# Hybrid encoder trunk on one core: in the first pass, the stores of operands and values move from SyncE's queue to ScalarE's

## The chip, the cores and the metric

The kernel runs on one core of one Trainium2 chip. The metric is the device time of one execution in microseconds (us), lower is better; the time of before is the median of 3 runs. The engines are TensorE (PE, with its weight loads PEld), VectorE (DVE), ScalarE (ACT), GpSimd (POOL) and SyncE (SP). SP only issues DMA transfers. ACT computes, and can issue them too.

## The reference, cut to what matters

One encoder layer, for a sequence of 2048 and one of 4096 tokens, width 1024:

```python
h = rms_norm(x, pre_g)
proj = einsum('bsd,de->bse', h, w_in)
a_u, a_v, a_gate, b_in, b_gate, c_in, c_gate = split(proj)
ya = mixer_a(a_u, a_v, ...) * silu(a_gate)   # v = layer_norm(gelu(a_v)), 128x128 mix of positions
yb = mixer_b(b_in, b_w, b_scale) * silu(b_gate)   # pooled means
yc = mixer_c(c_in, c_w) * silu(c_gate)   # 2-D Fourier transform
y = einsum('bse,ed->bsd', concat(ya, yb, yc), w_out)
out = x + rms_norm(y, post_g)
```

## The kernel before, in words

**Passes.** The 6144 tokens are 12 blocks of 512. The first pass (0 to about 505 us) takes block after block: it normalises x, projects the columns of a_v, c_in and c_gate, and writes three things to DRAM: the operands of the projections (`op_d`), the values gelu(a_v) (`vn_d`) and the Fourier input and gate (`z_d`, `gc_d`). The later passes read `op_d` and `vn_d` again for the B and A columns, and a last one makes the output. Only the first pass is touched here.

**A block of the first pass.** The 2x2 split of the projection is done with seven products instead of eight, in the order P1, P2, X1, X2, Y1, X3, Y2. Each product takes one operand of 128x1024, in two parts: ACT casts the high part (`p_P1h`, `p_X1h`, ..., L131; L807 in the first block), DVE or POOL subtracts it from the operand to get the low part (`p_P1l`, ..., L132; L805). PE multiplies them in three units (`Pc`, `Xc`, `Yc` twice, `Pg`, `Xg`, `Yg` once). ACT and DVE then evacuate the banks (`ks1c`, `ku2c`, `ku3c`, `s1g`, `cgt`), ACT does the gelu (`vg`, L743, L757) and the silu of the gate (`cgt`, L1003). There are buffers for three operand pairs.

**Where operands come from.** The four quarters of the next block's x (`xp_{b+1}_0..3`) are normalised in place by DVE (L608), after ACT has squared rows of x (`xrow`, L575) and DVE and PE have spread the factor (`diag`, `prb`, `rbc`). Sums and differences of quarters (L171 to L185) overwrite them for X1, X2, Y1, Y2. Each of the seven operands of a block is stored in full, 512 KB: P1, P2 and X3 by `normaliser` (L612), the others by `operands`, all through `keep_operand` (L599). That is 84 stores; the 48 stores of values (192 KB each) stand at L1002.

**What sets the order.** A scheduler places the instructions, except the start-up of block 0, whose order on PE, DVE, ACT and POOL is written out by hand (L829 to L915). Each engine takes its instructions in order, SP its DMAs too: one that must wait holds all behind it. Every DMA signals its end on one of eight semaphores (DMAHW0 to DMAHW7), given out in turn over all DMAs of the program, and waits on that semaphore before it is issued.

Of the kernel before, what the change touches and what calls it, by code (L numbers as in the profile page):

```python
# [15 lines left out]
P = 128  # L16
# [15 lines left out]
def hybrid_encoder(  # L32
# [33 lines left out]
    nc = tc.nc  # L66
# [40 lines left out]
    op_d = dpool.tile([NB, 7, P, 1024], F32, name="op_d")  # L107
    vn_d = dpool.tile([NTOK // P, P, 384], F32, name="vn_d")
# [12 lines left out]
    def chunk(b, c):  # L121


        return b // 2 * SB + c // 2 * TB + b % 2 * HB + c % 2 * P

    def in_seq(t):
        return (0, t) if t < SEQS[0] else (1, t - SEQS[0])
# [15 lines left out]
    OUT_ORDER = ("P1", "X1", "P2", "X2", "Y1", "X3", "Y2")  # L143
# [12 lines left out]
    def operands(quads, s1, make, order, sum_engines, prepare=None, store=None):  # L156

        a11, a12, a21, a22 = quads
        e = sum_engines
        src = {"P1": a11, "P2": a12, "X1": a11, "X2": a21, "Y1": s1, "X3": a22, "Y2": a12}  # L160
        for m in order:
            if m == "P1":
                if prepare:
                    prepare(0)
                op = make(a11, m)
                if prepare:
                    ins = last_split[0]
                    with tc.issue_after(getattr(ins, "ins", ins)):
                        for q in PREP:
                            prepare(q)  # L170
                e[0].tensor_add(s1, a21, a22)  # L171
                if store:
                    store("Y1", s1)
                yield op
                continue
            elif m == "X1" and order[0] == "P1":
                e[1].tensor_sub(a11, s1, a11)  # L177
                if store:
                    store("X1", a11)
            elif m == "X2":  # L180
                e[2].tensor_sub(a21, a22, a11)
                if store:
                    store("X2", a21)
            elif m == "Y1":
                e[3].tensor_sub(a12, a12, a11)  # L185
                if store:
                    store("Y2", a12)
            yield make(src[m], m)
# [3 lines left out]
    def make_operand(name, pool_lo=()):  # L192
        def make(src, m):
            hi = hpool.tile([P, 4, HB], F32R, tag="h", name=f"{name}_{m}h")
            lo = hpool.tile([P, 4, HB], F32R, tag="h", name=f"{name}_{m}l")
            last_split[0] = split(src.rearrange("p (k t) -> p k t", k=4), hi, lo, m in pool_lo)
            return hi, lo

        return make
# [292 lines left out]
    def run_background(n=1):  # L492
        while n > 0 and background:
            try:
                next(background[0])
                n -= 1
            except StopIteration:
                background.pop(0)
# [19 lines left out]
    def load_x(b, src, tagp):  # L518
        qs = []
        for q in range(4):  # L520
            t = xtile(f"x{tagp}_{b}_{q}")
            nc.sync.dma_start(t, src[b, q])
            qs.append(t)
        return qs
# [41 lines left out]
    def row_squares(b):  # L566

        ss = e0.tile([P, 2 * NCH], F32, tag="ss8", name=f"ss8_{b}", bufs=2)
        for c in range(NCH):
            t = e0.tile([P, D], F32, tag="xrow", name=f"xrow{b}_{c}", bufs=2)  # L570
            s, t0 = in_seq(chunk(b, c))
            nc.sync.dma_start(t, (x_sample, x_prompt)[s][t0 : t0 + P, :])
            for h in range(2):
                half = t[:, h * TB : (h + 1) * TB]
                nc.scalar.activation(half, half, AF.Square, accum_out=ss[:, 2 * c + h : 2 * c + h + 1])  # L575
        return ss

    def statistics(b, ss):

        two = ss.rearrange("p (c h) -> p c h", h=2)  # L580
        rr = rstd_rows(b, two[:, :, 0], two[:, :, 1])
        r = e0.tile([P, TB], F32, tag="rbc", name=f"rbc{b}", bufs=2)
        ps = bank(f"prb{b}")
        for a in range(2):
            diag = e0.tile([P, 2, P], F32, tag="diag", name=f"diag{b}_{a}", bufs=2)
            for c in range(2):
                nc.vector.tensor_scalar_mul(diag[:, c], ident, rr[:, 2 * a + c : 2 * a + c + 1])
            nc.tensor.matmul(
                ps[:, a * HB : (a + 1) * HB], full, diag.rearrange("p c t -> p (c t)"),
                start=True, stop=True, skip_group_check=True,  # L590
            )
        nc.scalar.copy(r, ps)  # L592
        return r[:, 0:HB], r[:, HB:TB]

    def keep_operand(b):


        def store(m, t):
            nc.sync.dma_start(op_d[b, OUT_ORDER.index(m)], t)  # L599

        return store

    def normaliser(b, xs, rbc):
        def normalise(q, ks=range(4)):
            a, kh = q // 2, q % 2
            for k in ks:
                sl = slice(k * HB, (k + 1) * HB)
                nc.vector.scalar_tensor_tensor(  # L608
                    xs[q][:, sl], xs[q][:, sl], g8_sb[:, 4 * kh + k : 4 * kh + k + 1],
                    rbc[a], ALU.mult, ALU.mult,  # L610
                )
            if 3 in ks and q != 2:  # L612
                keep_operand(b)(("P1", "P2", None, "X3")[q], xs[q])

        return normalise
# [11 lines left out]
    t = e0.tile([P, 2, P], F32, name="ident")  # L627
# [192 lines left out]
    def rest_of_weights(i):  # L820
        split_weights(("X2", "Y2", "Y1", "X3")[i])
        if i in (1, 2):
            for quads, eng in ((wv, nc.gpsimd), (cwq, nc.vector), (wcg, nc.gpsimd)):
                weight_sum(quads, i + 1, eng)
# [146 lines left out]
    for b in range(NB):  # L971
        blk = nblk
        if b + 1 < NB:
            nxs = load_x(b + 1, xt, "p")
            nblk = Block(b + 1)
        for i, m in enumerate(ORDER):
            op = ready.pop(0)
            if b > 0 or i > 2:
                blk.product(m, op)
            if b == 0 and 0 < i < 4:  # L980
                rest_of_weights(i)
            if b > 0 or i > 1:
                blk.after(m)
            if i < 5:
                if b > 0 or i > 0:
                    ready.append(next(stream))
            elif b + 1 < NB:
                if i == 5:
                    xs = nxs
                    stream = operands(  # L990
                        nxs, e1.tile([P, 1024], F32, tag="s3", name=f"s3_{b + 1}"), make_operand(f"p{b + 1}", ("X2", "X3")),
                        ORDER, SUMS0, normaliser(b + 1, nxs, nrbc), keep_operand(b + 1),
                    )
                ready.append(next(stream))
            if i == 0 and b + 1 < NB:
                nsq = row_squares(b + 1)
            if i == 2 and b + 1 < NB:
                nrbc = statistics(b + 1, nsq)
            if i in (1, 5):
                run_background(1)  # L1000
        for c in range(NCH):
            nc.sync.dma_start(vn_d[chunk(b, c) // P], blk.vf[c])  # L1002
        nc.scalar.activation(blk.cgts, blk.cgts, AF.Silu)  # L1003
        for a in range(2):
            s, t0 = in_seq(chunk(b, 2 * a))
            nc.sync.dma_start(
                gc_d[s][:, t0 : t0 + HB].rearrange("(j p) t -> p j t", p=P), blk.cgts[:, :, a * HB : (a + 1) * HB]
            )
# [356 lines left out]
    for q in range(NS):  # L1365
# [21 lines left out]
        for i, m in enumerate(OUT_ORDER):  # L1387
            op = ready.pop(0)
            if i == 2:
# [4 lines left out]
                for c in range(2):  # L1394
                    t = e3b.tile([P, D], F32, tag="xr", name=f"xr{q}_{c}", bufs=2)
# [32 lines left out]
            if q < NS - 1:  # L1428
                if m in ("X3", "Y2"):
                    c = 1 if m == "X3" else 0  # L1430
# [174 lines left out]
```

## Time and profile before

| | |
|---|---|
| median of 3 runs | 1875.86 us (1874.49 to 1877.32) |
| profiled execution, its own time | 1884.69 us |
| its span, first to last instruction | 1882.9 us |
| mean granted TensorE clock | 0.968 |
| PE, DVE, ACT, POOL busy | 93%, 76%, 50%, 48% of the span |

Times of rows are those of the profiled execution, which took 8.83 us more than the median. In the rows, `SPq` is SP issuing a DMA, `a <- b` reads "a waited for b", and `out<-in` names the tiles without their numbers.

### The profile page before, as it was taken

The page shows a single profiled execution, that of the slowest core. Times are in us where ns is not written, and L with a number is a line of the kernel's source. Part 1 is how long each engine was busy: PE and PEld are TensorE (multiplying, and loading weights), DVE is VectorE, ACT ScalarE, POOL GpSimd, SP SyncE. Part 2 cuts the span into 40 slices and gives each one's busy share as a digit, 9 for nine tenths or more (in the row PEclk, how much of TensorE's full clock was granted, in tenths as well). Part 3 has the DMA queues.
Part 4 walks back from the last instruction along what each step waited for, and adds up shares of the span by engine and source line. Part 5 has one row for each costly group of instructions (what it writes and reads, how often), then busy time and mean ns, then how long its engine had stood idle before and what let it go on. Part 6 is the DMA issues. An engine that isn't in the chain of part 4 may idle for free.

```text
span 1882.9 us, 28108 instructions
## 1 busy us (share of the span) xinstructions
PE 1743.8 (93%) x9784; PEld 1501.9 (80%) x9784; DVE 1425.7 (76%) x2215; ACT 935.7 (50%) x1718; POOL 907.2 (48%) x592
## 2 busy tenths in 40 slices
PE   4899999899788899999889998999959999999998
PEld 4899989899766688877668877878847888888886
DVE  8777777767379977987967567666677888888886
ACT  4556555433454454555555754575743333333332
POOL 6333456456554444444534332333435656566564
PEclk8999999999989999999899999999989999999999
DMA  9799998787688666566766577665755454545443
GB/s 337 273 305 319 343 335 311 247 291 256 226 296 274 241 217 234 182 213 223 254 231 240 201 249 240 232 215 193 257 176 179 162 170 158 169 161 170 158 148 119
DMA packets 212285, 433.35 MB, mean 230 GB/s; under 512 B 35504, under 2 KB 107824, under 8 KB 212144
## 3 DMA queue, kind: packets, MB, share of 16 engines
q1 hardware_dynamic: 212144, 431.56, 66.4%
q8 instruction: 77, 1.26, 0.3%
q14 instruction: 64, 0.52, 0.1%
HBM read 292.55 MB, written 145.23 MB: 233 GB/s over the span
## 4 chain that ended last, share of the span: by engine, by line
PE 52%; DVE 19%; DMA 12%; issue 7%; ACT 4%; POOL 4%; SPq 2%; POOLq 0%; DVEq 0%; ACTq 0%
PE Xo L135 3%; PE Xo L136 3%; PE Xo L137 3%; PE Po L137 2%; PE Po L136 2%; PE Po L135 2%; PE Yo L136 2%; PE Yo L137 2%; PE Yo L135 2%; PE Aa L136 2%; DVE xp L608 2%; PE Aa L137 2%; PE Aa L135 2%; DMA xrow<-in_x_sample 2%; PE pm L1252 2%
## 5 line engine op out<-in xcount | busy, mean ns | idle before, releaser
L1435 POOL TENSOR_TENSOR cc<-cc,xr 128x1024 f32<-128x1024 f32 x46 | 119.1, 2589 | 50.7 <-DVE cc L1434 50.7
L132 DVE TENSOR_TENSOR yo_P<-y,yo_P 128x512 fp32r<-128x512 f32 x48 | 121.8, 2538 | 0.1
L131 ACT CAST yo_X<-y 128x512 fp32r<-128x512 f32 x72 | 44.3, 616 | 146.4 <-POOL y L177 73.6
L608 DVE SCALAR_TENSOR_TENSOR xp<-xp,g_sb,rbc 128x256 f32<-128x256 f32 x192 | 108.3, 630 | 6.6 <-ACT rbc L592 4.1
L1376 ACT ACTIVATE junk<-cc 128x512 f32<-128x512 f32 x72 | 45.6, 633 | 87.7 <-DVE cc L1417 55.3
L132 DVE TENSOR_TENSOR yo_X<-y,yo_X 128x512 fp32r<-128x512 f32 x72 | 67.9, 942 | 20.1 <-ACT yo_X L131 20.1
L1232 ACT ACTIVATE vn<-vn,lnst 128x96 f32<-128x96 f32 x192 | 70.2, 454 | 23.0 <-DVE lnst L1227 22.8
L132 POOL TENSOR_TENSOR yo_Y<-y,yo_Y 128x512 fp32r<-128x512 f32 x24 | 31.6, 1315 | 93.9 <-ACT yo_Y L131 93.9
L1226 POOL TENSOR_TENSOR lnst<-lnst,mhalf 128x16 f32<-128x16 f32 x12 | 37.5, 3126 | 77.9 <-DVE lnst L1225 77.9
L171 POOL TENSOR_TENSOR s<-xp,xp 128x1024 f32<-128x1024 f32 x11 | 26.4, 2399 | 87.9 <-DVE xp L608 87.9
L1223 DVE BATCH_NORM_STATS2 lnst<-vn 128x6 f32<-128x96 f32 x192 | 35.9, 241 | 41.7 <-ACT vn L1232 31.2
L575 ACT ACTIVATE xrow<-xrow 128x512 f32<-128x512 f32 x88 | 54.6, 623 | 15.8 <-DMA xrow<-in_x_sample 12.8
L509 ACT COPY pa<-pb 32x512 f32<-32x512 f32 x36 | 22.3, 620 | 77.2 <-DVE pb L506 77.0
L1434 DVE SCALAR_TENSOR_TENSOR cc<-cc,orr,pgb 128x512 f32<-128x512 f32 x69 | 57.5, 861 | 3.2 <-POOL orr L1384 3.2
L135 PE MATMUL Po<-woP1h,yo_P 128*128 128x512 f32 x96 | 38.5, 401 | 17.3 <-ACT yo_P L131 17.3
L1252 PE MATMUL pm<-ws,vn 128*32 128x128 f32 x1152 | 44.7, 282 | 4.0 <-ACT vn L1232 4.0
L1252 PEld LDWEIGHTS pm<-ws,vn 128*32 128x32 f32 x1152 | 36.3, 113 | 14.0 <-ACT vn L1232 10.0
L135 PE MATMUL Yb<-b_Y2h,wbY2h 128*128 128x512 f32 x72 | 31.7, 441 | 16.5 <-DVE gb L265 12.6
L132 POOL TENSOR_TENSOR p_X3l<-xp,p_X3h 128x1024 fp32r<-128x1024 f32 x12 | 30.3, 2528 | 31.2 <-ACT p_X3h L131 26.3
L135 PE MATMUL Xc<-wtX1h,p_X1h 128*128 128x320 f32 x96 | 31.3, 327 | 14.9 <-ACT p_X1h L131 10.6
L1143 POOL COPY edge<-gb 128x8 f32<-128x8 f32 x36 | 18.5, 520 | 53.3 <-ACT gb L1181 53.3
L1272 ACT ACTIVATE ga<-ga 128x512 f32<-128x512 f32 x36 | 22.0, 628 | 43.7 <-DVE ga L267 36.0
(628 smaller groups left out, 7113.6 us busy)
## 6 DMA issues: line engine op xcount, KB each, us to landing
op_d<-xp SPq DMA_DIRECT2D x72, 512.0 KB, 5.2
mt<-const_m SPq DMA_DIRECT2D x56, 512.0 KB, 6.2
xp<-in_xt SPq DMA_DIRECT2D x48, 512.0 KB, 5.7
out<-cc SPq DMA_DIRECT2D x46, 512.0 KB, 2.9
xr<-in_x_sample SPq DMA_DIRECT2D x32, 512.0 KB, 4.1
xrow<-in_x_sample SPq DMA_DIRECT2D x28, 512.0 KB, 6.2
vn_d<-vg SPq DMA_DIRECT2D x48, 192.0 KB, 2.9
vn<-vn_d SPq DMA_DIRECT2D x48, 192.0 KB, 4.4
```

Source lines behind the costliest of these rows:

```text
L131: nc.scalar.copy(hi, src)
L132: return (nc.gpsimd if pool_lo else nc.vector).tensor_sub(lo, src, hi.bitcast(F32))
L135: nc.tensor.matmul(ps, lh, rh, start=first, stop=False, skip_group_check=True)
L136: nc.tensor.matmul(ps, lh, rl, start=False, stop=False, skip_group_check=True)
L137: nc.tensor.matmul(ps, ll, rh, start=False, stop=last, skip_group_check=True)
L575: nc.scalar.activation(half, half, AF.Square, accum_out=ss[:, 2 * c + h : 2 * c + h + 1])
L608: nc.vector.scalar_tensor_tensor(xs[q][:, sl], xs[q][:, sl], g8_sb[:, 4 * kh + k : 4 * kh + k + 1], rbc[a], ALU.mult, ALU.mult,)
L1232: nc.scalar.activation(v_, v_, AF.Identity, bias=nb[:, j : j + 1], scale=rv[:, j : j + 1])
L1252: nc.tensor.matmul(pm[32 * hd : 32 * hd + 32, c * P : (c + 1) * P], vn[c][:, 96 * hd + 32 * t : 96 * hd + 32 * t + 32], ws[:, hd], start=True,
L1376: nc.scalar.activation(junk, src, AF.Square, accum_out=ss[:, j : j + 1])
L1434: nc.vector.scalar_tensor_tensor(cc[c][:, hs], src, rr, pgb[:, hs], ALU.mult, ALU.mult)
L1435: nc.gpsimd.tensor_add(cc[c], cc[c], xr[c])
```

## The change

The engine that issues the DMA is another one at two places; what is stored, and where, stays.

```diff
         def store(m, t):
-            nc.sync.dma_start(op_d[b, OUT_ORDER.index(m)], t)
+            nc.scalar.dma_start(op_d[b, OUT_ORDER.index(m)], t)
...
         for c in range(NCH):
-            nc.sync.dma_start(vn_d[chunk(b, c) // P], blk.vf[c])
+            nc.scalar.dma_start(vn_d[chunk(b, c) // P], blk.vf[c])
```

So 132 of the DMA instructions leave SP's program and stand in ACT's. Three places follow. The first is ACT in the start-up, before and then with the change; `xp_0_114` and `xp_1_115` are the first two quarters of block 0, `sq` a square for its norm, `p_P1h` and `p_P2h` the high parts of its first two operands, and the brackets name the semaphores that a row waits for.

```order
L807 CAST p_P1h<-xp_0_114 128x512 [waits DVE_49]
L535 ACTIVATE sq_214<-xp_3_117 128x512
L807 CAST p_P1h<-xp_0_114 128x512 [waits DVE_49]
L689 CAST wgP2h<-cg_121 128x512 [waits DMAHW5_49]
L689 CAST wtP2h<-wv_138 128x4x192 [waits DMAHW4_49]
```

```order
L807 CAST p_P1h<-xp_0_114 128x512 [waits DVE_49]
L599 DMA op_d<-xp_0_114 128x1024 [waits DMAHW2_49,DVE_49]
L535 ACTIVATE sq_214<-xp_3_117 128x512
L807 CAST p_P1h<-xp_0_114 128x512
L689 CAST wgP2h<-cg_121 128x512 [waits DMAHW5_49]
```

The store of the first operand now stands between the two halves of that operand's own cast. In SP's order of before, the same store waits for the same DMAHW2, eight DMAs behind the load that used it last:

```order
L637 DMA cg_122<-in_w 128x512 [waits DMAHW2_49]
L922 DMA bw_496<-in_b_w 96x96 [waits DMAHW3_49]
L924 DMA bsc_498<-in_b_scale 96x96 [waits DMAHW4_49]
L1031 DMA wall_b<-in_w 128x512 [waits DMAHW5_49]
L1031 DMA wall_b<-in_w 128x512 [waits DMAHW6_49]
L1031 DMA wall_b<-in_w 128x512 [waits DMAHW7_49]
L964 DMA wall_a<-in_w 128x512 [waits DMAHW0_49]
L964 DMA wall_a<-in_w 128x512 [waits DMAHW1_49]
L599 DMA op_d<-xp_0_114 128x1024 [waits DMAHW2_49,DVE_49]
```

It is `cg_122`'s second load (L637), and it stands in the same place in SP's order with the change.

The second place is block 8 on ACT, from block 7's last gelu (`vg_1_3450`) to the cast of block 8's Y1 operand (`p_Y1h`), as the difference; `xp_0_3440` is block 8's first quarter and `xp_0_3882` block 9's, which DVE's L608 normalises in this stretch.

```order
 L743 ACTIVATE vg_1_3450<-ku2c_1_3625 128x192
-L752 COPY ks1c_0_3934<-Pc_0_3895 128x320
 L1003 ACT_TABLE_LOAD
 L1003 ACTIVATE cgt_3448<-cgt_3448 128x1024
+L1002 DMA vn_d<-vg_1_3450 128x384
+L599 DMA op_d<-xp_0_3440 128x1024
 L131 CAST p_X1h<-xp_0_3440 128x1024
```

```order
+L599 DMA op_d<-xp_1_3442 128x1024
+L599 DMA op_d<-xp_0_3882 128x1024
 L131 CAST p_Y1h<-s_8_3790 128x1024
```

Two stores stand ahead of `p_X1h`, and the store of block 9's first operand stands ahead of block 8's `p_Y1h`. On DVE in the same stretch, behind the normalisation of `xp_0_3882`:

```order
 L587 TENSOR_SCALAR diag_1_4518<-ident,rr_4510 128x128 x2
 L608 SCALAR_TENSOR_TENSOR xp_0_3882<-xp_0_3882,g_sb,rbc_4082 128x256 x4
+L132 TENSOR_TENSOR p_Y1l<-s_8_3790,p_Y1h 128x1024
 L755 TENSOR_TENSOR ku2c_0_4065<-Xc_0_4026,ks1c_0_3934 128x320
-L132 TENSOR_TENSOR p_Y1l<-s_8_3790,p_Y1h 128x1024
```

The low part of Y1, which reads `p_Y1h`, has moved ahead of the evacuation `ku2c_0`.

The third place is ACT at the start of the last block, with the change; `xp_0_4742` holds its X1 operand, `wbY1l` is a weight of the next pass that SP loads, and the numbers of the semaphores show who shares one.

```order
L1003 ACTIVATE cgt_4750<-cgt_4750 128x1024 [waits DVE_49]
L752 COPY ks1c_0_5204<-Pc_0_5165 128x320 [waits PE_49]
L599 DMA op_d<-xp_0_4742 128x1024 [waits DMAHW0_49,DVE_49]
L1002 DMA vn_d<-vg_1_4752 128x384 [waits DMAHW1_49,Activation_49]
L131 CAST p_X1h<-xp_0_4742 128x1024
L1036 CAST wbY1h<-wbY1l 128x1536
```

Before, `p_X1h` stood right behind `ks1c_0` there; now two stores are between them, and the last user of DMAHW0 ahead of the first is the load of `wbY1l`.

## Rows read from the trace of the kernel before

**Rows 1.** The page, part 1: busy time by engine.

```profile
PE 1743.8 (93%) x9784; PEld 1501.9 (80%) x9784; DVE 1425.7 (76%) x2215; ACT 935.7 (50%) x1718; POOL 907.2 (48%) x592
```

**Rows 2.** Busy time summed over eight windows, 0 to 550 us.

```profile
sum 550.00, PE 486.50 PEld 472.12 DVE 396.24 ACT 284.37 POOL 280.36; mean PE 60.81 PEld 59.02 DVE 49.53 ACT 35.55 POOL 35.05
```

**Rows 3.** PE's waits, 0 to 60 us: us in total, times, longest.

```profile
PE pss L551 <- DVE sq L542: 10.1, 2, 8.8
PE Xc L135 <- ACT wtX1h L689: 4.3, 1, 4.3
PE Xc L136 <- DVE wtX1l L692: 4.0, 1, 4.0
```

**Rows 4.** PE's waits, 60 to 505 us.

```profile
PE Xc L135 <- ACT p_X1h L131: 10.6, 5, 3.9
PE Xc L135 <- DVE ku2c L755: 5.5, 2, 5.3
PE prb L588 <- DVE diag L587: 3.8, 2, 2.4
PE Pc L135 <- ACT ks1c L752: 3.4, 2, 2.6
```

**Rows 5.** SP's waits, 12 to 31 us.

```profile
SPq L599 <- DMA cg<-in_w: 0.2, 1, 0.2
```

**Rows 6.** Tile cg, 12.0 to 12.6 us: ns min/median/max, first and last start.

```profile
L637 SPq DMA_DIRECT2D cg<-in_w x1: 578/578/578, 12.3 to 12.3; - x1
...
DMA to landing us min/median/max: 7.6/7.6/7.6
```

**Rows 7.** Tile op_d, first pass: the issues on SP.

```profile
L599 SPq DMA_DIRECT2D op_d<-xp x72: 319/408/3068, 19.9 to 485.6; - x72
```

**Rows 8.** Tile vn_d, first pass: the issues on SP.

```profile
L1002 SPq DMA_DIRECT2D vn_d<-vg x48: 319/442/1832, 89.3 to 512.2; - x48
```

**Rows 9.** Timeline of ACT, start-up: start, length, what.

```profile
15.31 0.62 ACT L535 ACTIVATE sq<-xp 128x512 f32<-128x512 f32 x1
15.84 0.60 ACT L807 CAST p_P1h<-xp 128x512 fp32r<-128x512 f32 x1
```

**Rows 10.** Timeline of DVE, start-up.

```profile
16.05 2.38 DVE L805 TENSOR_TENSOR p_P1l<-xp,p_P1h 128x512 fp32r<-128x512 f32 x2
18.36 1.76 DVE L541 TENSOR_TENSOR sq<-sq,sq 128x512 f32<-128x512 f32 x1
```

**Rows 11.** Timeline of ACT, blocks 6 to 7.

```profile
315.13 0.36 ACT L743 ACTIVATE vg<-ku2c 128x192 f32<-128x192 f32 x1 [1.17 <-DVE ku2c L772]
...
318.99 1.03 ACT L131 CAST p_X1h<-xp 128x1024 fp32r<-128x1024 f32 x1
```

**Rows 12.** Timeline of DVE, block 8.

```profile
366.89 5.78 DVE L608 SCALAR_TENSOR_TENSOR xp<-xp,g_sb,rbc 128x256 f32<-128x256 f32 x4
372.59 0.48 DVE L755 TENSOR_TENSOR ku2c<-Xc,ks1c 128x320 f32<-128x320 f32 x1
372.99 1.21 DVE L132 TENSOR_TENSOR p_Y1l<-s,p_Y1h 128x1024 fp32r<-128x1024 f32 x1
```

**Rows 13.** Timeline of ACT, block 8.

```profile
364.97 1.05 ACT L131 CAST p_Y1h<-s 128x1024 fp32r<-128x1024 f32 x1 [2.56 <-PE Pc L136]
```

**Rows 14.** Timeline of ACT, block 7.

```profile
330.79 1.05 ACT L131 CAST p_Y1h<-s 128x1024 fp32r<-128x1024 f32 x1 [3.45 <-PE Xg L136]
```

**Rows 15.** Tile Yc, block 7, 330 to 345 us.

```profile
L135 PE MATMUL Yc<-wtY1h,p_Y1h x8: 306/307/308, 337.4 to 340.4; 128*128 128x320 f32 x8
```

**Rows 16.** Tile wbY1l, 478 to 500 us.

```profile
L1035 SPq DMA_DIRECT2D wbY1l<-wall_b x1: 414/414/414, 481.4 to 481.4; - x1
...
DMA to landing us min/median/max: 6.0/6.0/6.0
```

**Rows 17.** Timeline of ACT, last block.

```profile
478.28 1.04 ACT L131 CAST p_X1h<-xp 128x1024 fp32r<-128x1024 f32 x1 [0.81 <-DVE xp L177]
```

**Rows 18.** Tile p_X1h, PE, last block.

```profile
L135 PE MATMUL Xc<-wtX1h,p_X1h x8: 304/308/311, 480.8 to 487.0; 128*128 128x320 f32 x8
```

**Rows 19.** SP's waits, 0 to 505 us.

```profile
SPq L599 <- DVE xp L608: 69.1, 20, 9.4
```

**Rows 20.** ACT's waits, 60 to 505 us.

```profile
ACT xrow L575 <- DMA xrow<-in_x_sample: 12.8, 11, 2.3
```

## The prediction

> **What bounds the kernel now.** I read the page's busy shares first. PE is busy 93% of the span and ACT 50% [rows 1]. The busy times by stretch say the same of the pass that is touched: PE 486.50 us of the first 550, ACT 284.37 [rows 2]. So PE sets the pace, and whatever reaches PE late lengthens the pass; ACT as a sum has room.
>
> Next, PE's waits, which say what reaches it late already. In the start-up PE waits for DVE's squares, then for weights from ACT and DVE (10.1, 4.3, 4.0 us) [rows 3]. From 60 to 505 us only some 26 us of waiting are left; the four largest are in [rows 4]. The largest is `p_X1h`, the cast on ACT that opens X1: 10.6 us in five blocks. None of these waits is for a load, and PE never waits for SP. The view shows which change would hurt: anything that makes ACT late at `p_X1h`, or holds DVE at `ku2c`.
>
> Then SP. It sits idle with a store of an operand at its head 69.1 us in all, because DVE has not yet normalised the quarter [rows 19]. That idle time costs nothing unless something behind it in SP's order is urgent. The same kind of wait is now put in ACT's order, where casts and evacuations stand behind it.
>
> **The change part by part.**
>
> *What is removed.* SP loses 132 issues of about 0.41 us [rows 7, 8], 132 x 0.41 = 54 us, and the waits at their head. For a gain somebody must have waited for a DMA that SP issued late. PE did not. ACT waited 12.8 us for rows of x [rows 20], which feed the normalisation of the next block, and DVE's `diag` and `ks1c` behind it cost PE 3.8 and 3.4 us [rows 4]. So the gain lies between 0 and 3.8 + 3.4 = 7 us. I take 0: those two rows name DVE and ACT, not a DMA.
>
> *Price of an issue on ACT.* The trace has no store issued by ACT. The nearest row is the same store on SP, 0.32 us at the least, 0.41 in the middle [rows 7]. I take 0.41. Eleven stores a block are 4.5 us of ACT in a block of some 40 us, which half-idle ACT can carry; what counts is where they stand, and what they wait for.
>
> *Start-up.* The first store stands between the halves of the cast `p_P1h`. It waits for DMAHW2, last used by the second load of `cg_122`. SP issued that load at 12.3 and it landed 7.6 us later, at 19.9 [rows 6]; the store was issued on SP at 19.9, its wait put down to just that load [rows 5, 7]. ACT would reach the store at 15.31, where the square stood [rows 9]. So ACT is held for 19.9 - 15.3 = 4.6 us, and 0.41 for the issue: 5.0 us. The second half of `p_P1h` ends at 15.84 + 0.60 + 5.0 = 21.4 instead of 16.4. DVE, which had both halves of `p_P1l` done at 18.43 [rows 10], finishes the second half (2.38 / 2 = 1.2 us) at 22.6: 4.2 us late, and the squares' sum (L541), the norms of the next quarters and PE's first products stand behind it. The next two stores hold ACT too, but ACT and their data now come later, so these holds lie mostly inside the 4.2. Two more issues stand right ahead of the second half of `p_X1h`, 0.8 us. Sum +5. Bounds: 0, if DVE's and PE's waits in [rows 3] (10.1 of them for squares) take it up, and 10, if a second hold of the same size adds up.
>
> *X1's cast in each block.* Between the last gelu of a block (315.13) and the next `p_X1h` (318.99) ACT runs without a gap [rows 11]. With the change two stores stand there, 0.8 us, and three more between the gelus, which had a gap of 1.17 us to hide them in [rows 11]. So `p_X1h` is 0.8 to 5 x 0.41 = 2.05 us late. Where PE already waits for it, in five blocks, all of that is lost; I take 1.2 us x 5 = +6, bounds 4 and 10. In the other six it has cover of a size that the rows don't give; 0 to 6 x 1 us, and I take 0.
>
> *The store of the next block's first operand.* In block 8 it stands ahead of `p_Y1h`. Its data are ready when DVE's norm ends, 366.89 + 5.78 = 372.67 [rows 12]; `p_Y1h` was cast at 364.97 [rows 13], and now follows at 372.67 + 0.41 = 373.1, ending at 374.1. On DVE `p_Y1l` now stands ahead of `ku2c_0`: it ends at 374.1 + 1.2 = 375.3, so `ku2c` starts at 375.3 instead of 372.59 [rows 12], 2.7 us late. PE waited 5.3 us for just this `ku2c` [rows 4], so +2.7 is lost in full. In some four other blocks the same store holds ACT as long (its 20 waits on SP reach 9.4 us [rows 19]), but `p_Y1h` has cover: in block 7 it was done at 331.8 [rows 14] and, with 1.2 us for the low part, 4.4 us ahead of Y1 at 337.4 [rows 15]. I take +0.3 each, together +4 for this part. Bounds: 2.7; and 2.7 + 4 x (9.4 - 4.4) = 23 if each is held for the longest wait.
>
> *The last block.* The X1 store waits for DMAHW0, last used by the load of `wbY1l`, which landed at 481.4 + 6.0 = 487.4 [rows 16]. `p_X1h` stood at 478.28 [rows 17] and PE used it from 480.8 [rows 18]. At worst the cast starts at 487.4 + 0.8 = 488.2, and PE gets it at 489.2, 8.4 us late. The change's order on SP has that load some rows earlier, so it lands earlier by an amount that no row shows: 0 to 8, and I take +4.
>
> *Sum.* 5 + 6 + 4 + 4 = +19 us on the profiled 1884.69 (span 1882.9): 1903.7. That execution was 8.83 us above the median, so on the scale of the runs 1903.7 x 1875.86 / 1884.69 = **1895 us**. Bounds of the terms: 0 + 4 + 3 + 0 = +7, and 10 + 10 + 6 + 23 + 8 = +57 together, which need not meet. The likeliest case's own range is +8 to +32, 1884 to 1908.
>
> **The rivals.**
>
> *No change.* ACT's holds fall into its idle half, and PE's waits grow by no more than 3 us. For it: ACT busy 284 of 550 us [rows 2], and 4.4 us of cover in block 7. Against it: the start-up and `ku2c` in block 8, where no cover is left. Time about 1877. The Trainium skill, "DMA: Bandwidth & Descriptors", section "Issuing engines are not separate DMA queues", speaks for this case: DMAs from any engine run on the same 16 DMA engines, and issuing from several saves only the time of the issue on the sequencer. By it the sum would be 0: SP's 54 us are saved where nobody waits. The trace agrees on the side of the gain (PE has no wait for a load); that issuing on ACT costs nothing, no row shows.
>
> *Faster.* The 69.1 us that SP idled behind unready operands vanish, so loads of x rows and small stores behind them go out earlier; the normalisation and `ks1c` come earlier, and PE gets back up to the 7 us worked out above. It decides if ACT finds the data and the semaphore of most stores free when it reaches them. 1884.69 - 7 is 1877.7, or 1869 on the scale of the runs. Against it: the scheduler put stores right behind their operand's norm, where data are last. The Trainium skill, "Perfetto Trace Analysis", section "DMA Optimizations", advises this: one DMA-capable engine for inputs, another for outputs. By its advice the sum would be negative; the order here keeps z_d and gate stores on SP, so it is half done at most.
>
> *Much slower.* The holds ahead of `p_Y1h` outrun their cover in most blocks, each PE wait lets the next block's casts slip, and the last block takes its full 8. Then +40, 1916. It decides if ACT's holds are typically over 5 us beyond cover, that is near 9.4 rather than 5.
>
> **How the numbers follow.** Likeliest, slower by 8 to 32 us: 0.52. Much slower: 0.21. No change: 0.15. Faster: 0.12. About 0.2%, 3.8 us, is what a measurement can tell from no change; by it, faster 0.12, same 0.14 and slower 0.74 (0.01 of the no-change case ends above). The range from 1873 to 1916 leaves out most of the faster case and the upper half of the much slower one, 2 in 10.
>
> **What would show it.** In the profile after: ACT idle ahead of L599, waiting for DVE's L608 and for DMAs of other tiles, some tens of us in the first pass; the first store on ACT at about 19.9 and the half of `p_P1h` behind it at about 20.3; PE's wait for `p_X1h` grown from 10.6 to about 17; `ku2c` in block 8 at 5.3 + 2.7; the stage up to 505 us longer by about 19, and later passes unchanged. It is wrong if ACT's waits at L599 are small, if PE's waits in the first pass stay at 26 us, or if PE's waits move to another line, such as Y1's operands.

## The result, and the profile after

The change made the kernel slower: 1894.98 us median of 6 runs (1890.07 to 1897.83), against 1876.3 us before (6 runs, 1872.66 to 1881.56). The ratio is 1.0095, 95% interval [1.0073, 1.0118], so between 14 and 22 us are lost.

The place is the first pass, as a view of one tile shows. These are the casts of the last operand of each block, `p_Y2h`, in the profile of before and then of after (ns min/median/max, then the start of the first and of the last in us).

```profile
L131 ACT CAST p_Y2h<-xp x12: 1037/1048/1057, 60.0 to 496.2; 128x1024 fp32r<-128x1024 f32 x12
```

```profile
L131 ACT CAST p_Y2h<-xp x12: 1036/1047/1054, 65.0 to 515.1; 128x1024 fp32r<-128x1024 f32 x12
```

Block 0 is 5.0 us late, block 11 18.9 us. (The casts of a second run of the same order, the control below, stand up to 1.8 us from those of before; smaller differences say nothing.) The profiled spans differ by less, 1891.7 against 1882.9. The profiled execution of before took 8.83 us more than its median, and part of that lies where nothing was changed: between 1100 and 1200 us its PE ran at a granted clock of 0.95 against 0.98 after, and there the distance of the two profiles shrinks by 5.5 us (casts of `a_P1h`: 14.4 us apart until 1083, 8.9 from 1235). So the block starts tell more than the span here.

The page of after: part 1, and of part 3 the queues. q10 is the new one, ACT's; before had no such line.

```profile
PE 1747.2 (92%) x9784; PEld 1505.1 (80%) x9784; DVE 1420.6 (75%) x2215; ACT 933.0 (49%) x1718; POOL 894.9 (47%) x592
...
q1 hardware_dynamic: 193136, 378.08, 58.8%
q10 hardware_dynamic: 19008, 53.49, 7.3%
```

Over the whole span no engine works more than 3.4 us longer [rows 1]. What grew are PE's waits in the first pass, from 26.3 us to 35.5 (60 us to its end); the largest of after, which answer to [rows 4]:

```profile
PE Pc L135 <- ACT ks1c L752: 16.8, 7, 3.7
PE Xc L135 <- ACT p_X1h L131: 8.7, 4, 4.6
PE Xc L135 <- DVE ku2c L755: 3.4, 1, 3.4
PE prb L588 <- DVE diag L587: 2.4, 1, 2.4
PE Yc L135 <- ACT p_Y1h L131: 2.0, 1, 2.0
```

The new wait is `ks1c`, 3.4 us before and 16.8 now. ACT copies the sum of P1 out of the bank into which PE then adds P2; PE's P2 (`Pc`) cannot go on before the copy. The copy stands behind the block's stores, gelus and silu on ACT. These waits are 9 of the 14 us that blocks 1 to 11 lose. The rest is in PE's busy time. Between the first and the last of the casts above, before and after (length, busy time of PE, its weight loads, DVE, ACT and GpSimd, then granted clock, DMA share and GB/s):

```profile
60.00:496.20 436.20, 409.73 (x2891) 404.01 (x2891) 317.30 (x480) 228.22 (x453) 221.96 (x108) 0.98 0.85 295
65.00:515.10 450.10, 414.52 (x2894) 409.49 (x2894) 313.99 (x481) 226.54 (x454) 213.37 (x108) 0.97 0.83 286
```

PE is idle for 9.1 us more and busy for 4.8 us more with the same work, at a lower granted clock. An instance of both is block 1. The operand of a store there is ready at 89.65 (GpSimd's L171), but on ACT the store waits on for the landing of a store of values. The gelu behind it reads none of that, and ACT stands idle for 5.17 us:

```profile
93.14 0.35 ACTq L599 DMA_DIRECT2D op_d<-s  x1
93.54 0.36 ACT L743 ACTIVATE vg<-ku2c 128x192 f32<-128x192 f32 x1 [5.17 <-DMA vn_d<-vg]
```

`p_X1h` follows at 98.38, and PE waits 4.6 us for it, until 99.48. From 100 to 102 us PE's granted clock then stands at the lower of its two levels (0.50), and block 1 ends 9.9 us late, 5.0 more than block 0. In block 7 the second `ks1c` itself stands behind a store whose operand DVE still normalises:

```profile
347.24 0.33 ACTq L599 DMA_DIRECT2D op_d<-xp  x1
347.61 0.42 ACT L752 COPY ks1c<-Pc 128x320 f32<-128x320 f32 x1 [8.24 <-DVE ku2c L755]
```

PE waits 3.2 us for it. Of the 16.8 us at `ks1c`, 7.7 stand behind such stores (blocks 2, 3, 4 and 7). The other 9.1, in blocks 9 to 11, stand behind a cast `p_P2h` that waits for the norm of its own operand, as it did before; there no store need be the cause.

The start-up, on ACT's timeline of after (start, length, what, idle time ahead of it and what ended it), answers to [rows 9]:

```profile
14.95 0.62 ACT L807 CAST p_P1h<-xp 128x512 fp32r<-128x512 f32 x1 [0.92 <-DVE xp L608]
20.53 0.34 ACTq L599 DMA_DIRECT2D op_d<-xp  x1
20.92 0.63 ACT L535 ACTIVATE sq<-xp 128x512 f32<-128x512 f32 x1 [5.34 <-DMA cg<-in_w]
21.45 0.60 ACT L807 CAST p_P1h<-xp 128x512 fp32r<-128x512 f32 x1
```

and DVE's of after to [rows 10]:

```profile
22.09 1.36 DVE L805 TENSOR_TENSOR p_P1l<-xp,p_P1h 128x512 fp32r<-128x512 f32 x1 [5.18 <-ACT p_P1h L807]
```

ACT reaches the first store at 15.6 and stands idle for 5.34 us, and the wait names a load that the square behind it does not read: `cg`, whose semaphore the store shares. DVE then waits 5.18 us for the second half of `p_P1h`, and ends its own second half at 23.45 instead of 18.43.

### The profile page after: what moved, and what is told of

Its sections match the earlier page's. It is cut to its first block, busy times and chain, and to the rows that moved or that the text cites. A ratio compares the mean times of both kernels' runs of the same rounds, so it can differ in the third digit from the quotient of the medians.

```text
span 1891.7 us, 28061 instructions
## 1 busy us (share of the span) xinstructions
PE 1747.2 (92%) x9784; PEld 1505.1 (80%) x9784; DVE 1420.6 (75%) x2215; ACT 933.0 (49%) x1718; POOL 894.9 (47%) x592
## 4 chain that ended last, share of the span: by engine, by line
PE 42%; DVE 11%; DMA 5%; issue 3%; ACT 3%; POOL 2%; SPq 1%; POOLq 0%; DVEq 0%; ACTq 0%
PE Xo L135 3%; PE Xo L137 3%; PE Xo L136 3%; PE Po L137 2%; PE Po L135 2%; PE Po L136 2%; PE Yo L137 2%; PE Yo L135 2%; PE Yo L136 2%; PE Aa L136 2%; PE Aa L137 2%; PE Aa L135 2%; PE pm L1252 1%; DMA yc_d<-gm 1%; PE Ab L136 1%
## 5 line engine op out<-in xcount | busy, mean ns | idle before, releaser
L608 DVE SCALAR_TENSOR_TENSOR xp<-xp,g_sb,rbc 128x256 f32<-128x256 f32 x192 | 99.6, 584 | 7.0 <-ACT rbc L592 5.5
L171 POOL TENSOR_TENSOR s<-xp,xp 128x1024 f32<-128x1024 f32 x11 | 26.4, 2403 | 112.7 <-DVE xp L608 84.5
L135 PE MATMUL Pc<-wtP2h,p_P2h 128*128 128x320 f32 x96 | 33.4, 348 | 16.8 <-ACT ks1c L752 16.8
L132 DVE TENSOR_TENSOR p_X1l<-xp,p_X1h 128x1024 fp32r<-128x1024 f32 x11 | 20.1, 1827 | 36.5 <-ACT p_X1h L131 36.5
L587 DVE TENSOR_SCALAR diag<-ident,rr 128x128 f32<-128x128 f32 x44 | 42.1, 1014 | 7.1 <-PE prb L588 4.8
L1252 PEld LDWEIGHTS pm<-ws,vn 128*32 128x32 f32 x1152 | 35.6, 111 | 13.4 <-ACT vn L1232 9.6
```

The source lines that it names most:

```text
L132: return (nc.gpsimd if pool_lo else nc.vector).tensor_sub(lo, src, hi.bitcast(F32))
L135: nc.tensor.matmul(ps, lh, rh, start=first, stop=False, skip_group_check=True)
L608: nc.vector.scalar_tensor_tensor(xs[q][:, sl], xs[q][:, sl], g8_sb[:, 4 * kh + k : 4 * kh + k + 1], rbc[a], ALU.mult, ALU.mult,)
L1252: nc.tensor.matmul(pm[32 * hd : 32 * hd + 32, c * P : (c + 1) * P], vn[c][:, 96 * hd + 32 * t : 96 * hd + 32 * t + 32], ws[:, hd], start=True,
```

## The experiments

All ratios are to runs of before on the same chip. The theory of the prediction is called holds: ACT stands at a store whose data or semaphore is not there, and what is behind it is late. Its rivals are the time of the issues themselves, two queues that disturb each other, and the order, since the scheduler places the instructions of PE, DVE and ACT anew in nearly every kernel.

**Which stores: operands alone, values alone.**

```diff
-            nc.sync.dma_start(op_d[b, OUT_ORDER.index(m)], t)
+            nc.scalar.dma_start(op_d[b, OUT_ORDER.index(m)], t)
```

> Only the 84 stores of operands go to ACT; the 48 of values stay on SP. Theory of holds (ACT waits at a store for data that DVE or POOL has yet to make, or for the DMA eight places earlier, and what stands behind it is late): the long holds belong to the operands, so most of the loss stays, 1888 to 1895 us against 1876.3 of before and 1895.0 of the change. Rival, issue time (each store costs ACT its 0.33 to 0.41 us, wherever it stands): 84 of 132 issues, 18.7 x 84/132 = +12, 1888 us. Rival, order (the scheduler puts PE, ACT and DVE into another order, and that order is worse): any time, since the order here is a third one.

Measured: 1.0084 [1.0069, 1.0100], within the interval of the whole change.

```diff
-            nc.sync.dma_start(vn_d[chunk(b, c) // P], blk.vf[c])
+            nc.scalar.dma_start(vn_d[chunk(b, c) // P], blk.vf[c])
```

> Only the 48 stores of values go to ACT. Theory of holds: their data come from ACT's own gelu, so only the semaphore can hold them: 0 to +4 us, 1876 to 1880. Issue time: 18.7 x 48/132 = +6.8, 1883 us. Order: any time.

Measured: 1.0001 [0.9989, 1.0013]. So 48 issues on ACT cost nothing that can be measured in the whole; a price per issue would have given 1.0036. The loss belongs to the operands. Within the first pass it is not as if nothing had happened: the order is another one, PE waits 9.5 us for `ks1c`, and the casts of `p_Y2h` are up to 9.9 us late (block 7) and 4.3 us in block 11.

**Block 0: the change without it, and it alone.** Here PE's order is that of the change, or of before, but for 9 lines.

```diff
-            nc.scalar.dma_start(op_d[b, OUT_ORDER.index(m)], t)
+            (nc.sync if b == 0 else nc.scalar).dma_start(op_d[b, OUT_ORDER.index(m)], t)
```

> The change, but the seven operand stores of block 0 stay on SP; the order of PE is that of the change but for 9 lines. Theory of holds: the hold of 5 us at the first store (ACT at 15.0, landing of the cg load at 20) goes, and with it the 5 us by which block 0 ended late: 1890 us. Issue time: 7 issues of 132, -1 us: 1894. Order: as the change, 1895.

Measured: 1.0053 [1.0034, 1.0072]. Against 1.0095 that is 0.42%, 8 us (the two intervals allow about 2 to 13), for seven stores of 132.

```diff
-            nc.sync.dma_start(op_d[b, OUT_ORDER.index(m)], t)
+            (nc.scalar if b == 0 else nc.sync).dma_start(op_d[b, OUT_ORDER.index(m)], t)
```

> Before, but the seven operand stores of block 0 go to ACT; the order of PE is that of before but for 9 lines. Theory of holds: block 0 ends 5 us late and nothing gives it back: 1881 us. Issue time: +1 us, 1877. Order: as before, 1876.

Measured: 1.0013 [1.0000, 1.0025], half of what I expected. Its casts of `p_Y2h` show why:

```profile
L131 ACT CAST p_Y2h<-xp x12: 1038/1047/1057, 64.6 to 495.0; 128x1024 fp32r<-128x1024 f32 x12
```

Block 0 is 4.6 us late, as in the change, but block 11 is 1.2 us early: blocks 4 and 5 gave the 4.6 back (its casts there are 1.9 and 0.5 us late). "Nothing gives it back" was wrong. Taken out of the whole change the start-up is worth about 8 us (2 to 13), put in alone about 2.4 (0 to 4.7); the two need not differ.

**Stores whose data are surely there.** The key experiment leaves block 0's operand stores on SP and the other 125 on ACT, but each operand store is queued behind the cast that reads the same operand.

```diff
-        nc.scalar.copy(hi, src)
+        last_cast[0] = nc.scalar.copy(hi, src)
...
+        def with_store(src, m):
+            op = make(src, m)
+            if behind:
+                ins = last_cast[0]
+                with tc.issue_after(getattr(ins, "ins", ins)):
+                    behind(m, src)
+            return op
...
```

> Block 0's operand stores on SP, all other 77 operand stores and the 48 of values on ACT as in the run of the change without block 0 (1.0053 of before), but each operand store stands right behind the ACT cast that reads the same operand, so its data are there when ACT reaches it; it can still wait for its semaphore. Theory of holds for data: nearly all of the +10 us goes, 1.000 to 1.002 of before (1878 to 1882 us). Rival, holds for semaphores: they stay, 1.004 to 1.006. Rival, time of the issues on ACT or two queues that disturb each other's transfers: 125 stores are still there, so 1.005 as before.

Measured: 0.9962 [0.9948, 0.9975], 1870.81 us. That is faster than before, which none of the theories of this run expected (the prediction's rival "faster" did), and 0.9% below the same stores on the same queue at the places that the scheduler chose. With the values back on SP:

> As the run at 0.9962 of before, but the 48 stores of values on SP. They stand behind ACT's own gelu, and moving them alone gave 1.0001. Theory of holds: nothing changes, 0.995 to 0.997. If SP's relief is what gains: a third of it goes, 0.9975.

Measured: 0.9951 [0.9934, 0.9968], 1869.11 us, the best of all. PE's waits in it, 60 to 505 us (its program is eight lines longer here, L760 is `ks1c`'s line):

```profile
PE Pc L135 <- ACT ks1c L760: 5.3, 3, 2.8
PE Xc L135 <- ACT p_X1h L131: 5.1, 6, 1.5
PE Xc L135 <- DVE ku2c L763: 3.9, 3, 1.8
PE prb L596 <- DVE diag L595: 2.4, 1, 2.4
```

`ks1c` is near the 3.4 us of before again (in the run at 0.9962 it was still 9.6), and `p_X1h` fell from 10.6 [rows 4] to 5.1. Where does a gain over before come from? The control has the stores at the same places of the program, but on SP:

> All 132 stores on SP as before, but the operand stores of blocks 1 to 11 stand in the program behind their own cast, as in the run that took 0.9962 of before. If that gain comes from ACT's queue (SP no longer idles with a store at its head, so its loads go out earlier): 1.000 of before here. If it comes from where the stores stand in the program (SP reaches no store before its data are there, other transfers pass): 0.996 here too.

Measured: 0.9992 [0.9978, 1.0006]; the order of PE, DVE and ACT is that of before, instruction for instruction. So the place in the program alone gains nothing; the gain comes with ACT's queue, or with the order that comes with it. SP's waits in it and then in the run at 0.9951 (0 to 505 us):

```profile
SPq L607 <- DVE xp L616: 69.7, 19, 10.0
SPq L752 <- DVE ku3c L774: 30.6, 12, 10.2
SPq L752 <- DVE ks1c L777: 15.4, 7, 4.6
SPq L580 <- ACT xrow L583: 8.2, 5, 3.6
```

```profile
SPq L752 <- DVE ku3c L774: 48.1, 20, 12.1
SPq L752 <- DVE ks1c L777: 34.7, 11, 4.5
SPq L769 <- ACT ztc L767: 27.9, 15, 4.9
SPq L580 <- ACT xrow L583: 22.0, 13, 3.5
```

The 69.7 us at the head of SP's queue (the operand stores, L607 here) are gone; SP now waits for small stores and free `xrow` buffers instead, that is, it is ahead of its work. That fits a relief of SP. It does not prove it, because the order differs too, and the run meant to tell them apart did not:

```diff
+            if b > 0:
+                nc.scalar.dma_start(mark_d[b, OUT_ORDER.index(m)], ones[:, 0:1])
...
```

> All stores on SP as in the run at 0.9992 of before, and besides 77 small DMAs of 512 bytes on ACT, one behind each operand's cast, which write a mark to DRAM. They make the scheduler choose another order of PE, ACT and DVE (about as far from before's as those of the two runs near 0.995), but take nothing off SP. If the gain of those runs comes from the stores that SP no longer has at its head: 1.000 of before or a little above. If it comes from the order: near 0.995 or anywhere else, since the order is again a new one.

Measured: 1.1617 [1.1589, 1.1645], for a reason of its own. The marks are 77 writes of 4 bytes in each of 128 partitions. Their landing times (min/median/max) were 7.2/12.2/18.0 us, and those of the operand stores beside them rose as well, here in this run's view of `op_d`:

```profile
DMA to landing us min/median/max: 2.7/11.8/22.5
```

That view counts some loads of `op_d` too; of the stores of `xp` alone, the pages have 12.4 us here and 5.2 before. ACT's and PE's waits grow with the landings: ACT waits 68.2 us for rows of x (12.8 before [rows 20]), PE 75.2 us for `ks1c` and 67.1 for `p_X1h`. It says what late landings do, and nothing of the order.

The block starts say more of where the gain lies. In the run at 0.9951 `p_Y2h` of block 11 is 8.4 us earlier than before, and block 8 alone gains 7.6. PE's wait of 5.3 us for `ku2c` there, which the prediction counted on, is gone. DVE's norm ahead of `ku2c` took 5.78 us before [rows 12] and 5.79 in the control, with GpSimd busy beside it almost throughout; here it took 2.78 in two parts, and GpSimd stood idle from 365.4 to 367.2. But block 8 gains as much without any relief of SP: 7.1 us in the run with the values alone, and 4.8 in the run below that leaves P1, P2 and X3 on SP. In those two SP idles 85.7 and 81.3 us at operand stores. So most of the gain lies in the new order of block 8 and in how DVE's work meets GpSimd's there. That SP's relief gains anything is not shown, though ACT's waits for rows of x do fall, from 15.9 us in the control to 7.2 here.

**Which operand stores.** My next idea was that the stores of normalised operands (P1, P2, X3) make the loss, since the longest waits named DVE's L608.

```diff
+            (nc.sync if b == 0 or m in ("P1", "P2", "X3") else nc.scalar).dma_start(op_d[b, OUT_ORDER.index(m)], t)
```

> As the change, but block 0's operand stores and, in the later blocks, the stores of P1, P2 and X3 (whose data DVE's normalisation makes) stay on SP: 44 operand stores and 48 of values on ACT. Holds for data: the long waits at ACT's stores name DVE's normalisation, so most of the +10 us goes: 1.000 to 1.002 of before. Issue time: 92 of 132 issues, 18.7 x 92/132 = +13, 1.007. Semaphores: two thirds of the stores still wait for one, 1.003.

Measured: 1.0094 [1.0074, 1.0113]. The idea falls: without these stores, and without block 0's, the loss is as large as that of the whole change, and larger than with them (1.0053), which holds alone do not explain. PE's largest wait, and ACT's waits that come from a store, in this run:

```profile
PE Pc L135 <- ACT ks1c L752: 24.0, 8, 6.7
```

```profile
ACT vg L743 <- DVE xp L177: 7.2, 2, 4.5
ACT vg L743 <- DMA wb_d<-wbo: 6.6, 1, 6.6
ACT vg L743 <- POOL s L171: 6.1, 1, 6.1
ACT L757 <- POOL xp L185: 4.4, 1, 4.4
```

The gelus `vg` (and their table load, L757) do not read what L177, L171 or L185 make, nor `wb_d`; the stores of X1, Y1 and Y2 ahead of them do, or share a semaphore with it. The holds were merely somewhere else. The inverse, only these stores on ACT, and not block 0's:

```diff
+            (nc.sync if b == 0 or m not in ("P1", "P2", "X3") else nc.scalar).dma_start(op_d[b, OUT_ORDER.index(m)], t)
```

> As before, but the 33 stores of P1, P2 and X3 of blocks 1 to 11 go to ACT, nothing else. Holds for data: they alone make most of the loss behind block 0, +5 to +10 us, 1.003 to 1.005 of before. Issue time: 33 of 132 issues, +4.7, 1.0025. Semaphores: a quarter of the stores, +2.5, 1.0013.

Measured: 1.0042 [1.0027, 1.0057], as expected of holds. Either set alone costs 0.4 to 0.9%; the two do not add up.

This run also sets the rival "order" aside at one place. Its order differs little from that of before, and from 266 to 313 us (before's time) it is the same, instruction for instruction, on PE, DVE, ACT and GpSimd. The second `ks1c` of block 6, first before, then in this run with the norm and the store ahead of it:

```profile
287.90 0.44 ACT L752 COPY ks1c<-Pc 128x320 f32<-128x320 f32 x1
```

```profile
283.15 7.78 DVE L608 SCALAR_TENSOR_TENSOR xp<-xp,g_sb,rbc 128x256 f32<-128x256 f32 x4
290.96 0.33 ACTq L599 DMA_DIRECT2D op_d<-xp  x1
291.37 1.28 ACT L757 ACT_TABLE_LOAD   x1 [7.03 <-DVE ku2c L755]
293.04 0.45 ACT L752 COPY ks1c<-Pc 128x320 f32<-128x320 f32 x1
```

The store goes out when the norm ends, at 290.93 (the row names `ku2c`, which starts at the same time). ACT has stood idle for 7.03 us, `ks1c` comes 5.1 us later than before although this run was about 1 us ahead, and PE waits 3.7 us for it; before it did not wait there. PE's granted clock, 1.00 throughout before, is at 0.50 from 292 to 298 us. `p_Y2h` is 1.5 us early in block 5 and 5.3 late in block 6: one hold costs 6.8 us, more than half of it as PE's wait and most of the rest as the lower clock.

**Another queue, and all of it behind the casts.** The 125 stores on GpSimd's queue:

> Block 0's operand stores on SP, the other 125 stores from GpSimd's queue instead of ACT's. Holds: GpSimd is held in ACT's place; it is 47% busy and PE waited for it only 0.5 us, so 1.000 to 1.003 of before, unless its sums for X2, X3 and Y2 come late. A second queue as such (two queues disturb each other's transfers, or a store goes out too early and delays a load): as with ACT, 1.005.

Measured: 1.0161 [1.0144, 1.0179]. GpSimd is held as ACT was, with the stores waiting for data (its waits, 60 to 540 us):

```profile
POOL op_d L599 <- DVE xp L608: 74.9, 24, 10.2
POOL vn_d L1002 <- ACT vg L743: 54.3, 14, 11.1
```

An issue on GpSimd also took longer, 0.56 us in the middle. How much is holds and how much is GpSimd's own, this run does not tell.

All 132 stores on ACT, block 0's behind their casts too:

```diff
     part_operand(xs[0], op1, k23, False)
+    keep_operand(0)("P1", xs[0])
...
```

> All 132 stores on ACT, as in the change, each operand store behind its own cast, block 0's too. Holds for data are gone; the first store still waits for the landing of the cg load at about 20. The half of p_P1h is then ahead of it. Theory of holds: the start-up loses under 1 us, 0.996 to 0.997 of before, with as many stores on ACT as in the change. Issue time: 1.009. If the semaphore's hold costs as much behind the cast as ahead of it: 0.9985.

Measured: 1.0057 [1.0034, 1.0080], between the two expectations. The start-up part came out:

```profile
17.34 0.60 ACT L813 CAST p_P1h<-xp 128x512 fp32r<-128x512 f32 x1
19.91 0.34 ACTq L607 DMA_DIRECT2D op_d<-xp  x1
20.29 0.62 ACT L695 CAST wgP2h<-cg 128x512 fp32r<-128x512 f32 x1 [2.35 <-DMA wall_b<-in_w]
```

ACT is still held until 19.9, but now the second half of `p_P1h` is ahead of the store, and block 0's `p_Y2h` starts at 60.7, 0.6 late. The loss comes later: `p_Y2h` is 5.9 us late in block 1, and over the pass PE waits 3.4 us each for `u3g` and `u2g` and 3.7 for `p_X1l`, all made by DVE. No hold of ACT names itself there. In block 1 the trace shows what happens instead. DVE's subtraction `wtX3l` starts at 60.15, 1.1 us later than before, and now just behind the start of GpSimd's `p_X3l` (60.06, 2.36 us) instead of ahead of it: it takes 3.08 us against 0.94. `u3g` behind it comes at 63.56 instead of 60.87, PE waits 3.4 us for it, and PE's granted clock is 0.57 from 64 to 72 us, against 0.79 before. So holds are not all: a shift of 1 us between DVE and GpSimd cost as much as a hold. How much of the 0.57% is of this kind, this run does not tell.

## Why the prediction was right, and where it was not

**Outcome.** The forecast, slower by 8 to 32 us around 1895, held: 1894.98. That the centre fits so well is luck: the terms behind it are partly wrong and cancel, and two things that it priced nowhere, PE's lower clock behind a wait and the changed meeting of DVE and GpSimd, are in the measured time too.

**Start-up, +5: right, with its mechanism.** The hold was 5.34 us against 5.0, DVE ended `p_P1l` 5.0 late against 4.2, and block 0 was 5.0 late. What was missed is that later blocks can return it: alone it cost 2.4 us (0 to 4.7).

**"Price of an issue on ACT", 0.41 us each: the step that failed.** ACT's timeline of after, block 8:

```profile
375.14 1.06 ACT L1003 ACTIVATE cgt<-cgt 128x1024 f32<-128x1024 f32 x1
375.30 0.33 ACTq L599 DMA_DIRECT2D op_d<-xp  x1
376.11 1.03 ACT L131 CAST p_X1h<-xp 128x1024 fp32r<-128x1024 f32 x1
```

The store is issued while the silu runs, and the cast follows the silu without a gap. An issue that needs not wait is hidden behind the instruction ahead of it; the values on ACT (1.0001) and the 77 to 125 stores of the two best runs say the same. So "+6 at X1's cast" was mis-sized: `p_X1h` cost 8.7 us, less than the 10.6 of before. In its place `ks1c` rose by 13.4 us. The holds were there, but they also made late the copy that PE's P2 waits for; I had not priced it. The prediction's own sign of being wrong, waits of PE that move to another line, came true here. And where `p_X1h` was late, the price was not that of issues: 4.6 of its 8.7 us are block 1's, behind a store that waited for a semaphore.

**Block 8's `ku2c`, +2.7, and the other holds ahead of `p_Y1h`.** The mechanism was right, but the place was off by one instruction. ACT's timeline of after:

```profile
388.68 0.33 ACTq L599 DMA_DIRECT2D op_d<-xp  x1
389.05 1.04 ACT L131 CAST p_Y1h<-s 128x1024 fp32r<-128x1024 f32 x1 [7.25 <-DVE xp L608]
```

ACT idled 7.25 us for the norm, then cast `p_Y1h`. PE waited 2.0 us for the cast itself and 0.3 for its low part, not at `ku2c`. DVE's norm took 2.72 us there instead of 5.78 [rows 12], so block 8 gained 4.1 us on before instead of losing 2.7: a part of the loss elsewhere is hidden by it. In block 7, where the prediction gave `p_Y1h` cover, the store held ACT for 8.24 us and made `ks1c` late.

**The last block, +4: wrong.** The semaphore came from the load of `wbY1l`, as said, but that load went out at 490.3 and landed 5.7 us later, at 496.0. The store followed it at 496.13, while the silu (495.84, 1.06 us) still ran:

```profile
495.84 1.06 ACT L1003 ACTIVATE cgt<-cgt 128x1024 f32<-128x1024 f32 x1
496.13 0.33 ACTq L599 DMA_DIRECT2D op_d<-xp  x1
496.81 0.41 ACT L752 COPY ks1c<-Pc 128x320 f32<-128x320 f32 x1
```

This store cost nothing. (PE's 3.7 us for `ks1c` in this block have the wait for the norm ahead of `p_P2h` behind them, as said.) Together the terms behind block 0 were +14 and block 11 came 18.9 - 5.0 = 13.9 later: right in sum, wrong in place, and so luck.

**The gain, 0 to 7 us, taken as 0.** In the change no time is gained, though what the rival "faster" began with did happen: the 12.8 us for which ACT waited for rows of x [rows 20] are gone. With each store behind its cast the time is 9 us below before (0.9951). The rival had named the condition, that ACT finds data and semaphore free at most stores, and it was not met in the change. But its mechanism is not shown by that gain, because 7.6 us of it fall in block 8, which gains as well where SP is not relieved.

**"No change", by the Trainium skill.** The Trainium skill, "DMA: Bandwidth & Descriptors", section "Issuing engines are not separate DMA queues", was right in its own matter: the second queue as such did not speed the transfers up (median landing of the stores of `xp` 5.0 us after, 5.2 before; of the smaller `vn_d` stores 4.7 after, 2.9 before). It does not speak of what the issuing engine does behind the DMA. The Trainium skill, "Perfetto Trace Analysis", section "DMA Optimizations", says that it may make sense to give loads to one engine and stores to another, above all with loops. Here this came out 0.5% faster with each store behind an instruction that had already waited for its data, and 0.95% slower without.

**Open.** That holds cost time is shown, by block 0, by block 1 of the change and by block 6 of the run at 1.0042, where the order is that of before. How the loss of the whole change divides is not: what share the order has in every run where PE's order differs (only the two block-0 runs and the control share an order with another run throughout), and how much of the holds is data and how much semaphores. The rivals "issue time" and "two queues", as the cause of the loss, fall with the values alone and the two best runs.

## What to carry to other kernels

A DMA in the queue of a computing engine costs little by itself, but it stands in that engine's order: ask what it waits for, data and semaphore, and what stands behind it. Place it behind an instruction of the same engine that already waited for the same data; with all but block 0's operand stores at such places the kernel was 0.5% faster, most of it by the order that came along, and at the scheduler's own places it was 0.95% slower. When judging what lateness costs, follow the copies that free or continue a bank, not only the casts that feed the next product, and add what PE's lower clock behind the wait costs. Before crediting a gain to the change, look in which block it lies, and whether runs without the change have it there too.

## What the runs showed of the hardware that was not expected

- ACT issues a DMA while its previous instruction still runs: 0.33 us in the shadow of a 1.06 us silu, no gap behind it.
- 77 writes of 128 x 4 bytes, 0.04 MB in all, went with a median landing of the 512 KB stores of `xp` of 12.4 us instead of 5.2. From 100 to 200 us the 16 DMA engines were then busy throughout (a share of 1.07) at 185 GB/s, against 281 to 347 GB/s in the windows of before between 60 and 340 us, and the kernel took 16% longer.
- An issue took 0.33 us on ACT in the middle, 0.41 on SP [rows 7] and 0.56 on GpSimd.
- Towards the end of a wait of PE of 3.7 us (until 293.5), in an order that stayed the same, its granted clock fell to the lower level and stood there for about 6 us (0.50 from 292 to 298 us); before, without that wait, it stood at 1.00.
- The same subtraction on DVE (`wtX3l`, 128x768) took 0.94 us when it began 0.4 us ahead of a subtraction on GpSimd, and 3.08 us when it began 0.1 us behind one.
